# A hybrid decoder layer on one core: a quarter of memory and the spread of ln_g given to GpSimd's queue, other tiles for the first pair, another planning estimate

## The chip, the core and the metric

The kernel runs on one core of one Trainium2 chip, in one launch. The metric is the device time of one execution in microseconds (us). A profiled execution gives the span from the first to the last instruction and a trace of every engine: TensorE (PE, with its weight loads as PEld), VectorE (DVE), ScalarE (ACT), GpSimd (POOL) and SyncE (SP), which only issues transfers.

## The reference, cut to what matters

One pre-norm layer over x (1024 tokens x 2048), all in float32:

- h = RMSNorm(x) * ln_g; P = h @ W_in (2048 x 6672), its columns divided among three groups.
- Group A: chunked causal gMLP gating. Group B: a gated DeltaNet with 8 heads of 128, with a short convolution on q, k, v and a chunked delta rule (64 tokens a chunk), which needs the inverse of a unit lower triangular matrix for each chunk. Group C: cross-attention into 256 memory tokens (4 heads x 128), where m = RMSNorm(mem) * mem_norm_g and the keys and values are m @ w_mem_kv (2048 x 1024).
- Each group's output is multiplied by SiLU of its own gate columns; x + concat(A, B, C) @ W_out; and a final RMSNorm with final_g.

## The kernel before, in words

**Arithmetic.** Every large product is made of three fp32r products of parts: each operand is split into a rounded part and a rest ("hi" by a ScalarE copy, "lo" by a VectorE subtraction, `split_to`, line 440), and `triple` multiplies hi*hi, hi*lo and lo*hi into one PSUM bank. Part of the projections is made from seven products in place of eight of half-size blocks (`seven`, line 1286).

**Order.** All operations are first recorded in a plan (`Plan`, from line 50). `add` finds dependences by tile and region; `price` (from line 180) gives each operation a cost and, for a transfer, a latency `o.lat` behind its last byte; `issue` (line 228) then replays a list schedule with these estimates and emits the instructions of each engine in the order of their estimated start. The chip runs each engine's instructions in that fixed order and waits on semaphores for data. `rank` sets a priority, `behind(op)` lets the planner place an operation only after another one; it is no wait on the chip. As all instructions are emitted from one line, every row of the profile names L295.

**Start.** The memory's 256 rows come in two row tiles (`mem_rows`, kT and qT tiles) of four column quarters of 128x512 each; `load_mem(q)` (line 493) loads quarter q of both. `load_kv(k)` loads row block k of w_mem_kv (512 KB) into one of four buffers: two `wraw`, two `ut`. `spread_mem(q)` (line 539) transposes a quarter on TensorE and splits it into gt (hi) and inv (lo). The loop over k = 0..15 (from line 585) then multiplies block k, scaled by mem_norm_g, into the key banks (acc, 256 columns wide) and the value banks (dn, 512 wide). Between these steps the rows of x come in, are squared and summed, scaled by ln_g (`prep`, line 555, reads the gain tiles `gb`, which lie in the `zg` tiles) and transposed.

The loads at the start are issued in this order on SP's queue: quarter 0 of memory, weight block 0 in two halves, block 1, quarter 1, blocks 2 and 3, quarters 2 and 3. ln_g comes as four rows of 1x512 on ScalarE's queue, and `spread_gain` (line 550) multiplies each with a row of ones on TensorE to spread it over 128 partitions, and copies the bank to `gb` on ScalarE.

**First pair.** After the projections of the first DeltaNet heads, `blocks(0, ...)` starts the seven-product stage. It works in pairs of row blocks: the left operand is loaded into a buffer of `araw` (line 1247) by `loaded`, the right one into `wraw2`, and they are split into `ah4`/`al4` and `whi3`/`wlo3` (line 1249). `raws` lies on tiles of the projections (alo1), `whi`/`wlo` are the tiles that the projections' weights use, `zh`/`zl` lie on the `zg` tiles. The E tiles (two, 128x512) are used before by the DeltaNet's decay matrices.

**Scans.** `inverse` (line 957) makes the triangular inverses of 4 head pairs in 31 steps on VectorE, writes them to DRAM (`tdrearly`, `udrearly`) by GpSimd's queue; `levels` (line 984) reads blocks of them back by GpSimd's queue into `tblk` and `ut` and joins them by small TensorE products (dn<-tblk,gt and dn<-ut,y). Such operations stand between the large products of the seven-product stage.

Of the kernel before, what the change touches and what calls it, by code (L numbers as in the profile page):

```python
# [10 lines left out]
F32R = mybir.dt.float32r  # L11
# [6 lines left out]
P = 128  # L18
# [4 lines left out]
HT = 512  # L23
# [37 lines left out]
class Plan:  # L61
# [27 lines left out]
    @contextmanager  # L89
    def rank(self, cls):  # L90
        old, self.cls = self.cls, cls
        yield
        self.cls = old

    @contextmanager
    def behind(self, op):
        old, self.gate = self.gate, op
        yield
        self.gate = old
# [87 lines left out]
    def price(self, o, name, outs, ins):  # L187

        out = outs[0]
        n = math.prod(out.shape[1:])  # L190
        both = [*outs, *ins]
        psum = any(i.space == PSUM for i in both)
        pointer = any(i.shape[-1] == 1 and math.prod(i.shape[1:]) == 1 for i in ins[1:])
        o.moves = o.lock = 0
        o.lat = 0.0
        if name == "dma_start":
            o.cost = {"sp": 440.0, "act": 430.0, "pool": 550.0}[o.eng]
            src = ins[0]
            run = 4 * min(out.shape[-1], src.shape[-1])
            fixed, byte = self.PACKET  # L200
            o.moves = 4 * math.prod(out.shape) / run * (fixed + byte * run) / self.QUEUES
            if o.eng == "pool":
                o.lat = 1500.0
            elif out.space == DRAM:
                o.lat = 3000.0 if run < 512 else 1500.0
            elif list(src.ap)[0][0] == 0:
                o.lat = 3500.0
        elif o.eng == "pe":
            passes = 1 if ins[0].dtype == F32R else 2 if name == "transpose" else 4
            o.cost = max(13.3 + n / 2.4 * passes, 222.0 if passes == 4 else 110.0) if out.shape[0] == P else 30.0  # L210
            o.lat = 175.0
        elif o.eng == "act":
            o.cost = (165.0 if psum else 200.0) + 0.82 * n + (105.0 if pointer else 0.0)
            o.cost += 190.0 if "accum_out" in o.kw else 0.0
        elif o.eng == "dve":
            n = max([n] + [math.prod(i.shape[1:]) for i in ins])
            o.cost = (n + 151) / 0.96 + (60.0 if pointer and name == "scalar_tensor_tensor" else 0.0)
            o.lock = not psum and (name.startswith("tensor_") or name == "scalar_tensor_tensor")
            o.lock = o.lock and name != "tensor_reduce"
        else:  # L220
            o.lock = 1
            if name in ("memset", "affine_select"):
                o.cost = 100.0 + 0.83 * n * (1 if name == "memset" else 1.4)
                o.lat = 800.0 if name == "affine_select" else 0.0
            else:
                o.cost = 750.0 + 150.0 * (n - 1) if n < 8 else 200.0 + 2.1 * n
# [72 lines left out]
def kernel(  # L299
# [21 lines left out]
    x, mem, w_in, out = x[0], mem[0], w_in[0], out[0]  # L321
# [7 lines left out]
    V, S, G, PE, Q = R.dve, R.act, R.pool, R.pe, R.sp  # L329
    rank, behind = R.rank, R.behind  # L330

    def C(shape, name, dt=F32):
        return sb.tile(list(shape), dt, name=name, tag=name)[:]
# [31 lines left out]
    def heir(old, name, tag, n=4 * HT, dt=F32):  # L365

        t = sb.tile([P, n], dt, name=name, tag=tag)[:]
        R.users[t.tensor.name] = []
        R.heir[t.tensor.name] = old.tensor.name
        return t  # L370
# [23 lines left out]
    kvhi, kvlo = [*whi.bufs], [*wlo.bufs]  # L394
# [4 lines left out]
    ring = {t: Slots(t, 4, [P, HT]) for t in ("kT", "qT", "vs", "kd", "ai")}  # L399
# [3 lines left out]
    zgb = ring["zg"].bufs  # L403
# [23 lines left out]
    ident, ones, utri = (C([P, P], n) for n in ("ident", "ones", "utri"))  # L427
# [55 lines left out]
    def row_tiles(tag):  # L483
        if tag in ("inv", "gt", "ut"):
            return [b[:, i * HT : (i + 1) * HT] for b in (ring[tag](), ring[tag]()) for i in range(2)]
        return [ring[tag]() for _ in range(4)]

    gb = [ring["zg"]() for _ in range(4)]
    kvraw += [ring["ut"]() for _ in range(2)]
    mem_rows = [row_tiles("kT"), row_tiles("qT")]  # L490
    x_rows = {}

    def load_mem(q):
        for mt in range(2):
            Q.dma_start(mem_rows[mt][q], mem[mt * P : (mt + 1) * P, q * HT : (q + 1) * HT])

    def kv_parts(k):
        n = XW if k == 0 else 2 * XW
        return [slice(i, i + n) for i in range(0, 2 * XW, n)]

    def load_kv(k):
        for sl in kv_parts(k):
            Q.dma_start(kvraw[k % 4][:, sl], w_mem_kv[k * P : (k + 1) * P, sl])
# [10 lines left out]
    with rank(2):  # L514
        load_mem(0)
        S.dma_start(mrow, mem_norm_g[0].rearrange("(c p) -> c p", p=P))
        for c in range(4):
            S.dma_start(gb[c][0:1], ln_g[0:1, c * HT : (c + 1) * HT])
        for k in range(4):
            load_kv(k)  # L520
            if k == 1:
                load_mem(1)
    with rank(3):
        load_mem(2)
        load_mem(3)
# [4 lines left out]
    def spare():  # L530
        turn["dn"] = 1 - turn["dn"]
        return flip[turn["dn"]]

    pt = spare()
# [4 lines left out]
    def spread_mem(q):  # L539
# [6 lines left out]
            with rank(2):  # L546
                split_to(h[:, :, sl], l[:, :, sl], tok(tp), V)
        return h, l

    def spread_gain(c, pt):  # L550
        PE.matmul(pt, ones[0:1], gb[c][0:1], start=True, stop=True)
        with rank(3):
            S.copy(gb[c], pt)

    def prep(tt, put, bank):

# [28 lines left out]
    kvmark = []  # L585
    mhl = [spread_mem(0)]
    mhl.append(spread_mem(1))
    for k in range(KT):
        mh, ml = mhl[k // 4]
        if k >= 4:  # L590
            with rank(3):
                load_kv(k)
        hi, lo = kvhi[k % 2], kvlo[k % 2]
        with rank(2):
            for sl in kv_parts(k):
                raw = kvraw[k % 4][:, sl]
                S.activation(hi[:, sl], raw, AF.Copy, scale=gcol[:, k : k + 1])
                V.scalar_tensor_tensor(lo[:, sl], raw, gcol[:, k : k + 1], hi[:, sl], op0=ALU.mult, op1=ALU.subtract)
        kk = k % 4
        for h in range(NX):  # L600
            sl = slice(h * P, (h + 1) * P)
            triple(ka[h][:, :NMEM], (hi[:, sl], lo[:, sl]), (mh[:, kk], ml[:, kk]), k == 0, k == KT - 1)
        for mt in range(2):
            sl = slice(mt * P, (mt + 1) * P)
            triple(va[mt], (mh[:, kk, sl], ml[:, kk, sl]), (hi[:, XW:], lo[:, XW:]), k == 0, k == KT - 1)
        kvmark.append(R.ops[-1])
        if 1 < k < 6:
            spread_gain(k - 2, spare())
        if k in (3, 7):
            mhl.append(spread_mem(k // 4 + 2))  # L610
        if k == 1:
            load_x(0, "vs", kvmark[1:2] * 4)
        if k == 4:
            load_x(1, "kd", kvmark[4:5] * 4)
        if k == 5:
            prep(0, put0(0), spare)
            for mt in range(2):
                rm.append(C([P, 1], f"rm{mt}"))
                V.tensor_copy(rm[mt], row_scale(mem_rows[mt]))
        if k == 7:  # L620

            dg, rmb = (ring["E"]()[:, 0:NMEM] for _ in range(2))
            for mt in range(2):
                V.tensor_scalar(dg[:, mt * P : (mt + 1) * P], ident, rm[mt], None, op0=ALU.mult)
            pt = spare()
            PE.matmul(pt[:, 0:NMEM], ones, dg, start=True, stop=True)
            S.copy(rmb, pt[:, 0:NMEM])
        if k == 9:
            prep(1, put0(1), spare)
            load_x(2, "kT", (kvmark[6], kvmark[7], kvmark[7], kvmark[8]))  # L630
        if k == 13:
            load_x(3, "qT", (kvmark[10], kvmark[11], kvmark[11], kvmark[12]))
            with rank(2):
                prep(2, put0(2), spare)
# [37 lines left out]
    pt = dnr()  # L672
# [44 lines left out]
    def over(bufs):  # L717
        r = Ring("", 0, None)
        r.bufs = bufs
        return r  # L720
# [524 lines left out]
    ob = over(obs)  # L1245
    more = halves(ywide[3])
    araw = over([[t] for t in (*raws, more[0])])
    wraw2 = over([*kvraw[:2], more[1]])
    whi3 = over([*kvhi, heir(zgb[0], "zh", "zg0", 2 * HT, F32R)])
    wlo3 = over([*kvlo, heir(zgb[1], "zl", "zg1", 2 * HT, F32R)])  # L1250
    kept = [[ring[tag](slot=k) for k in range(2)] for tag in ("kT", "qT", "kd", "ai")]
    vs01 = [ring["vs"](slot=k) for k in range(2)]
    for tag in ("kT", "qT", "vs", "kd", "ai"):
# [9 lines left out]
    def load2(ts, src):  # L1263

        for i, x_ in enumerate(src):
            t = ts[i] if len(ts) == 2 else ts[0][:, i * HT : (i + 1) * HT]
            Q.dma_start(t, x_)
        return ts
# [49 lines left out]

    def loaded(src):
        with rank(4):  # L1320
            raw = load2(araw(), src)
        return split2(raw, ah4(), al4())

    def h_left(m, js):
# [456 lines left out]
```

## Time and profile before

| what | value |
|---|---|
| median of 3 runs | 1645.29 us (lowest 1644.62, one run at 8354.71) |
| the profiled execution's own time | 1643.28 us |
| its span | 1641.5 us |
| granted TensorE clock, mean | 0.997 |
| PE busy | 1616.7 us, 98% |
| DVE, ACT, POOL busy | 1258.1, 1031.8, 292.6 us |
| DMA | 427.89 MB, 261 GB/s mean |

Busy time of PE is the time in which at least one matmul is in flight. A matmul's row gives its start and the time until it leaves the array; matmuls overlap, so the distance between two starts, and not the duration, is what one more of them costs. A row of the waits names the engine that waited, what it waited for, the total, how often, and the longest.

### The profile page before, as it was taken

What the parts mean: (1) busy time and instruction counts of PE and PEld (TensorE: products, weight loads), DVE (VectorE), ACT (ScalarE), POOL (GpSimd) and SP (SyncE); (2) the same over time, 40 slices, a digit from 0 to 9 for tenths busy, and PEclk for the clock granted to TensorE, in tenths of its full rate; (3) what the DMA queues carried; (4) which work ended last, traced back from release to release, by engine and by line L of the source; (5) the groups of instructions that cost most, each with busy time, mean ns of one, the idle gap of its engine ahead of it and who ended that gap; (6) DMA issues with size and microseconds to landing.
All of it is one profiled execution on the core that took longest, in us unless ns stands there. A gap on an engine that the chain in (4) does not pass through costs nothing.

```text
span 1641.5 us, 26099 instructions
## 1 busy us (share of the span) xinstructions
PE 1616.7 (98%) x8570; PEld 1354.2 (83%) x8570; DVE 1258.1 (77%) x2081; ACT 1031.8 (63%) x2226; POOL 292.6 (18%) x482
## 2 busy tenths in 40 slices
PE   8999999999999999999999999999999999999997
PEld 6888888887788888888888888888888888888886
DVE  4856777779756668899998887677767788789775
ACT  5957675765465457977775357676656775344345
POOL 0101220351442010313244053301000000000001
PEclk9999999999999999999999999999999999999999
DMA  7887798898986787689888896698788769688646
GB/s 254 255 228 192 224 307 256 240 298 309 352 278 209 258 278 228 209 269 351 287 267 262 291 289 228 195 305 305 251 287 269 241 211 352 221 266 303 219 144 240
DMA packets 278579, 427.89 MB, mean 261 GB/s; under 512 B 30830, under 2 KB 104103, under 8 KB 278443
## 3 DMA queue, kind: packets, MB, share of 16 engines
q1 hardware_dynamic: 255682, 365.76, 68.4%
q0 software_dynamic: 22144, 59.40, 11.6%
q8 instruction: 67, 1.10, 0.3%
q10 hardware_dynamic: 616, 1.07, 0.2%
q14 instruction: 70, 0.57, 0.1%
HBM read 338.52 MB, written 87.06 MB: 259 GB/s over the span
## 4 chain that ended last, share of the span: by engine, by line
PE 81%; DMA 5%; DVE 2%; issue 2%; POOL 1%; ACT 1%; SPq 0%; POOLq 0%; DVEq 0%; ACTq 0%
PE acc L295 62%; PE dn L295 19%; DMA raws<-h0d 1%; DMA el<-vd 1%; DMA pd<-y 1%; DMA tdrearly<-inv 0%; DVE y L295 0%; DMA tblk<-mixd 0%; DMA late<-qT 0%; POOL inv L295 0%; DMA tblk<-tdrearly 0%; DMA ut<-udrearly 0%; DMA y<-in_w_in_dram 0%; DMA vs<-od 0%; DVE inv L295 0%
## 5 line engine op out<-in xcount | busy, mean ns | idle before, releaser
L295 PE MATMUL acc<-ahi,wlo 128*128 128x512 f32 (+1 forms) x1152 | 451.6, 392 | 1.0 <-DVE wlo L295 1.0
L295 PE MATMUL acc<-ahi,whi 128*128 128x512 f32 (+1 forms) x1152 | 449.6, 391 | 1.2 <-ACT whi L295 1.2
L295 PE MATMUL acc<-alo,whi 128*128 128x512 f32 (+1 forms) x1152 | 450.1, 391 | 0.0
L295 PEld LDWEIGHTS acc<-ahi,whi 128*128 128x128 f32 x1152 | 216.6, 188 | 42.4 <-ACT whi L295 1.6
L295 PEld LDWEIGHTS acc<-ahi,wlo 128*128 128x128 f32 x1152 | 216.8, 188 | 41.5 <-DVE wlo L295 1.4
L295 PEld LDWEIGHTS acc<-alo,whi 128*128 128x128 f32 x1152 | 216.7, 188 | 41.1
L295 PE MATMUL acc<-ahi,zh 128*128 128x512 f32 x736 | 232.2, 394 | 0.0
L295 ACT CAST whi<-wraw 128x512 fp32r<-128x512 f32 (+1 forms) x170 | 137.0, 808 | 111.3 <-PE acc L295 85.2
L295 DVE TENSOR_TENSOR wlo<-wraw,whi 128x512 fp32r<-128x512 f32 (+1 forms) x170 | 156.9, 924 | 61.3 <-ACT whi L295 54.9
L295 DVE TENSOR_TENSOR alo<-raws,ahi 128x1024 fp32r<-128x1024 f32 x131 | 159.9, 1221 | 35.9 <-ACT ahi L295 35.5
L295 ACT CAST ahi<-raws 128x1024 fp32r<-128x1024 f32 x131 | 137.3, 1048 | 65.3 <-PE dn L295 28.1
L295 PEld LDWEIGHTS acc<-ahi,zh 128*128 128x128 f32 x736 | 136.7, 188 | 26.9
L295 PE MATMUL acc<-ahi,zl 128*128 128x512 f32 x368 | 144.3, 392 | 0.0
L295 POOL TENSOR_TENSOR small<-small,mhalf 128x1 f32<-128x1 f32 x26 | 17.3, 671 | 591.2 <-DVE small L295 591.1
L295 DVE TENSOR_TENSOR ahi<-y,ahi 128x1024 fp32r<-128x1024 f32 x65 | 79.4, 1221 | 15.3 <-ACT ahi L295 15.2
L295 ACT CAST ahi<-y 128x1024 fp32r<-128x1024 f32 x65 | 68.1, 1048 | 29.9 <-PE dn L295 11.4
L295 PEld LDWEIGHTS acc<-ahi,zl 128*128 128x128 f32 x368 | 69.2, 188 | 13.7
L295 ACT CAST zh<-wraw 128x1024 fp32r<-128x1024 f32 x36 | 37.8, 1050 | 44.2 <-PE acc L295 36.0
L295 DVE TENSOR_TENSOR wlo<-y,whi 128x1024 fp32r<-128x1024 f32 x34 | 41.6, 1223 | 24.8 <-ACT whi L295 23.3
L295 PE MATMUL dn<-wlo,ahi 128*128 128x512 f32 x152 | 59.0, 389 | 0.0
L295 PE MATMUL dn<-whi,alo 128*128 128x512 f32 x152 | 59.0, 389 | 0.0
L295 PE MATMUL dn<-whi,ahi 128*128 128x512 f32 x152 | 58.8, 389 | 0.0
(410 smaller groups left out, 3299.9 us busy)
## 6 DMA issues: line engine op xcount, KB each, us to landing
wraw<-in_w_in_dram SPq DMA_DIRECT2D x268, 256.0 KB, 3.8
raws<-sd SPq DMA_DIRECT2D x148, 256.0 KB, 4.2
y<-in_w_in_dram SPq DMA_DIRECT2D x92, 256.0 KB, 4.7
y<-sd SPq DMA_DIRECT2D x77, 256.0 KB, 4.2
wraw<-in_w_out_dram SPq DMA_DIRECT2D x64, 256.0 KB, 4.2
raws<-h0d SPq DMA_DIRECT2D x54, 256.0 KB, 5.2
y<-in_w_out_dram SPq DMA_DIRECT2D x33, 256.0 KB, 4.6
sd<-zg SPq DMA_DIRECT2D x32, 256.0 KB, 4.7
```

The costliest lines, as they stand in the source:

```text
L295: o.fn(*o.args, **o.kw)
```

## The change

Five edits:

1. Quarter 1 of memory is loaded from GpSimd's queue, as its first instructions, in place of SP's fifth and sixth transfers.
2. The four 1x512 loads of ln_g on ScalarE's queue, the eight TensorE products and the four ScalarE copies that spread them are gone. Four transfers on GpSimd's queue, each reading 512 elements for 128 partitions, fill `gb` instead; the planner may place them only behind step k = 2.
3. The first pair's left operand goes into the two E tiles; later pairs use `araw` as before, so each of its buffers is met one pair later.
4. The hi and lo tiles of the right operands rotate in another order: the `zg` tiles (zh, zl) first, then the second and the first of the projections' tiles.
5. The planner's latency of a transfer on GpSimd's queue is 2500 ns in place of 1500.

The diff, whole:

```
@@ price
             if o.eng == "pool":
-                o.lat = 1500.0
+                o.lat = 2500.0
@@ loads
-    def load_mem(q):
+    def load_mem(q, queue=Q):
         for mt in range(2):
-            Q.dma_start(mem_rows[mt][q], mem[mt * P : (mt + 1) * P, q * HT : (q + 1) * HT])
+            queue.dma_start(mem_rows[mt][q], mem[mt * P : (mt + 1) * P, q * HT : (q + 1) * HT])
@@ start
         load_mem(0)
         S.dma_start(mrow, mem_norm_g[0].rearrange("(c p) -> c p", p=P))
-        for c in range(4):
-            S.dma_start(gb[c][0:1], ln_g[0:1, c * HT : (c + 1) * HT])
+        load_mem(1, G)
         for k in range(4):
             load_kv(k)
-            if k == 1:
-                load_mem(1)
@@ spread_gain
-    def spread_gain(c, pt):
-        PE.matmul(pt, ones[0:1], gb[c][0:1], start=True, stop=True)
-        with rank(3):
-            S.copy(gb[c], pt)
@@ loop over k
         kvmark.append(R.ops[-1])
-        if 1 < k < 6:
-            spread_gain(k - 2, spare())
+        if k == 2:
+            with rank(2), behind(kvmark[-1]):
+                for c in range(4):
+                    G.dma_start(gb[c], ln_g[0, c * HT : (c + 1) * HT].partition_broadcast(P))
@@ first pair
     araw = over([[t] for t in (*raws, more[0])])
+    first_raw = [ring["E"].bufs]
     wraw2 = over([*kvraw[:2], more[1]])
-    whi3 = over([*kvhi, heir(zgb[0], "zh", "zg0", 2 * HT, F32R)])
-    wlo3 = over([*kvlo, heir(zgb[1], "zl", "zg1", 2 * HT, F32R)])
+    whi3 = over([heir(zgb[0], "zh", "zg0", 2 * HT, F32R), *kvhi[::-1]])
+    wlo3 = over([heir(zgb[1], "zl", "zg1", 2 * HT, F32R), *kvlo[::-1]])
@@ loaded
-            raw = load2(araw(), src)
+            raw = load2(first_raw.pop() if first_raw else araw(), src)
```

## The prediction

> **What bounds the kernel now.** I read the page first, then the chain, then PE's waits, then stretches of 41 us, and at last the timeline where PE stands.
>
> ```profile
> span 1641.5 us, 26099 instructions
> PE 1616.7 (98%) x8570; PEld 1354.2 (83%) x8570; DVE 1258.1 (77%) x2081; ACT 1031.8 (63%) x2226; POOL 292.6 (18%) x482
> ```
> ```profile
> PE dn L295 <- DMA y<-in_mem_norm_g_dram: 4.2, 1, 4.2
> PE acc L295 <- ACT whi L295: 1.4, 2, 1.2
> PE dn L295 <- DMA ut<-udrearly: 1.4, 1, 1.4
> PE dn L295 <- DMA kT<-in_mem_dram: 1.4, 2, 1.1
> PE dn L295 <- DVE ai L295: 1.3, 2, 1.0
> PE acc L295 <- DVE wlo L295: 1.2, 2, 1.0
> PE dn L295 <- ACT ut L295: 1.1, 1, 1.1
> PE dn L295 <- DVE ut L295: 1.0, 1, 1.0
> PE acc L295 <- ACT gt L295: 0.9, 1, 0.9
> PE acc L295 <- DVE tn L295: 0.8, 1, 0.8
> PE dn L295 <- DMA el<-vd: 0.6, 1, 0.6
> PE dn L295 <- DMA tblk<-tdrearly: 0.6, 2, 0.3
> ```
> ```profile
> 0.00:41.00 41.00, 34.50 (x182) 28.39 (x182) 18.17 (x25) 23.86 (x42) 1.91 (x10) 0.96 0.76 254
> 41.00:82.00 41.00, 40.59 (x282) 36.42 (x281) 35.35 (x61) 38.87 (x81) 4.99 (x8) 1.00 0.89 255
> 1599.00:1640.00 41.00, 34.06 (x151) 27.88 (x149) 24.26 (x40) 23.75 (x40) 4.81 (x8) 0.95 0.70 252
> ```
>
> PE is busy for 1616.7 of 1641.5 us. All its idle time is 24.8 us: 4.2 before the first transfer lands, 6.9 at the end (41.0 less 34.06, the last row), and some 13 in short waits. So the ceiling is low: what shortens the kernel is matmul work taken away, or one of these waits; everything else must stay hidden. The columns of the stretches are length, busy us of PE, PEld, DVE, ACT and POOL, clock, DMA share and GB/s. After the first stretch PE hardly waits, so a lead won at the start is carried to the end, as long as ACT (38.87 of 41 us in the second stretch) follows.
>
> **The change part by part.**
>
> *Spreading ln_g (edit 2).* It goes from PE and ACT. On ACT the four copies and four issues lie beside PE's work and are counted as nothing; they only give ACT some room.
>
> ```profile
> 15.45 1.98 PE L295 MATMUL dn<-zg,ones 1*128 1x512 f32 x4
> 17.36 0.39 PE L295 MATMUL acc<-gt,whi 128*128 128x256 f32 x1
> L295 PE MATMUL dn<-zg,ones x8: 587/587/692, 15.5 to 32.2; 1*128 1x512 f32 x8
> ```
> ```profile
> 14.64:18.05 3.41, 3.41 (x13) 1.73 (x12) 1.28 (x1) 2.22 (x3) 0.00 (x0) 1.00 0.95 376
> 18.05:21.46 3.41, 3.41 (x18) 3.41 (x17) 0.00 (x0) 0.01 (x1) 0.00 (x0) 0.50 0.67 203
> 21.46:24.87 3.41, 3.41 (x22) 3.02 (x22) 0.69 (x1) 1.15 (x1) 0.00 (x0) 1.00 0.74 262
> ```
>
> The first four hold PE from their start to the next product, 17.36 - 15.45 = 1.91 us; there are eight: **-3.8**. PE's waits name no other operand at this place, so nothing else keeps PE there. Right behind the first four the granted clock falls to 0.50 for 3.41 us, and is 1.00 before and after. At half clock that stretch does 1.7 us less work. The stretch before it holds only 13 matmuls, among them the four that use one row of the array. Whether it is these that lower the clock, the trace doesn't say: the price lies between 0 and -1.7. I take **-1.7**, as the stretch without such products (21.46 to 24.87) has the full clock.
>
> *GpSimd's six transfers (edits 1, 2).* In the built order the two memory loads are GpSimd's first instructions, and the four loads of ln_g follow its memsets with no wait ahead of them: the planner holds them back behind k = 2, the chip does not. So 6 x 256 KB, 1.57 MB, run beside SP's first loads, of which 1.05 MB are new.
>
> ```profile
> L295 POOL DMA_DIRECT2D late<-kT x16: 539/546/607, 139.7 to 845.1; - x16
> 1.19 0.29 POOL L295 TENSOR_SCALAR_AFFINE_SELECT ident<-ident 128x128 f32<-128x128 f32 x1
> E<-gcd POOLq DMA_DIRECT2D x16, 256.0 KB, 7.2
> L295 DVE SCALAR_TENSOR_TENSOR vs<-vs,small,zg x4: 744/748/752, 32.9 to 36.5; 128x512 f32<-128x512 f32 x4
> 10.80 1.09 PE L295 MATMUL dn<-ident,kT 128*128 128x128 f32 x4 [1.12 <-DMA kT<-in_mem_dram]
> ```
> ```profile
> 0.00:4.20 4.20, 0.00 (x0) 0.00 (x0) 0.00 (x0) 0.00 (x0) 1.35 (x9) 1.00 0.42 108
> 4.20:7.61 3.41, 2.23 (x9) 1.71 (x10) 1.29 (x3) 3.02 (x5) 0.00 (x0) 1.00 0.95 309
> 7.61:10.77 3.16, 2.08 (x6) 1.35 (x6) 2.20 (x4) 1.72 (x2) 0.00 (x0) 1.00 0.86 274
> 10.77:15.45 4.68, 4.65 (x20) 4.19 (x20) 1.98 (x3) 1.17 (x2) 0.00 (x0) 1.00 1.04 410
> ```
>
> Two issues of 0.55 us (the first row: the time that one holds GpSimd) delay the identity, ready at 1.48, to 2.6. Its first user waits until 4.2, so this costs nothing; without that cover, 1.1. The gains land some 7 us behind issue (as E<-gcd, the nearest broadcast) at about 13, needed at 32.9: hidden.
>
> Memory and weights are another matter. Length times rate of the rows, added up, gives 0.45 MB moved by 4.2 us, 1.5 by 7.61, 2.4 by 10.77 and 4.3 by 15.45. If both queues take equal turns, the first weight half (the third of SP's 256 KB loads, 0.79 MB with it) lands when 1.57 MB have moved, at about 7.9; its split takes 0.7, and the first product starts near 8.9 in place of 7.61. But the wait of 1.12 us for quarter 1 is gone, and four transposes of it (1.1 us) come ahead of that product. PE's work in the two last rows, 2.08 + 4.65 less these 1.1, ends at 8.9 + 5.6 = 14.5, against 15.45 now. Quarter 2 stands behind 2.6 MB of SP's and all of GpSimd's, 4.2 MB: at 15.2, some 0.7 late for where the built order wants it. I take **0** for the sum of both. Bounds: -1.4 (the two waits for kT vanish, nothing else is late) and +3.4 (the 1.05 new MB at 309 GB/s, all ahead of PE).
>
> [...]
>
> *First pair (edits 3, 4).*
>
> ```profile
> 353.41 0.41 DVE L295 TENSOR_TENSOR ai<-dn,E 128x256 f32<-128x256 f32 x1
> 378.09 1.77 SPq L295 DMA_DIRECT2D raws<-h0d  x4
> 384.61 1.05 ACT L295 CAST ahi<-raws 128x1024 fp32r<-128x1024 f32 x1 [1.56 <-DMA raws<-h0d]
> 386.34 0.39 PE L295 MATMUL acc<-alo,whi 128*128 128x512 f32 x1
> 386.57 0.39 PE L295 MATMUL acc<-ahi,wlo 128*128 128x512 f32 x1
> 388.12 0.50 PE L295 MATMUL acc<-ahi,whi 128*128 128x512 f32 x1 [1.17 <-ACT whi L295]
> 390.81 0.50 PE L295 MATMUL acc<-ahi,wlo 128*128 128x512 f32 x1 [1.02 <-DVE wlo L295]
> ```
>
> Today the first pairs' left operands are loaded at 378.09, when PE has left alo1, land at 384.61, and PE waits 1.17 and 1.02 us for the splits. The E tiles are last read at 353.41 + 0.41, so the new wait of SP's queue for them, with weights behind it, costs nothing at the place where the built order has the two loads (the second near 356); if it came early, every weight behind would be late by as much. One pair is 24 products at 0.23 us (386.57 less 386.34), 5.4 us, enough to cover the second pair's splits, which arrive as now. **-2.2**, bounds -2.2 and 0.
>
> *Estimate (edit 5).* It moves what reads GpSimd's transfers behind other work. In the built order 244 products of 512 columns, in place of 185, stand between the first pair and the first product on tblk: 59 x 0.23 = 13 us more room.
>
> ```profile
> L295 DVE TENSOR_TENSOR alo<-raws,ahi 128x1024 fp32r<-128x1024 f32 x131 | 159.9, 1221 | 35.9 <-ACT ahi L295 35.5
> ```
>
> The inverse on DVE gets three more such splits (1.2 us each) and a few half-size sums between its steps, some 6 us. So 7 us of room meet waits of 1.4 and 0.6 (ut, tblk): **-1.9**, bounds -1.9 and 0. The other waits (ai 1.3, ACT ut 1.1, DVE ut 1.0, tn 0.8, el 0.6: 4.8) are dealt anew; I take no change, bounds -4.8 and +4.8.
>
> **Sum.** -3.8 - 1.7 + 0 - 2.2 - 1.9 = -9.6. The profiled execution's own time is 1643.28 (span 1641.5 and 1.8 around it): 1633.7. The median of the runs lies 2.0 above it, at 1645.29: **1635.7 us**, 0.6% less, which counts as no change: about 2% (33 us) is what a measurement of this kernel can tell.
>
> **Rivals.**
>
> *Transfers in turn.* The new bytes come ahead of the weights, +3.4, and PE, waiting longer in the first 15 us, also gets no better clock (0 for 1.7): -3.8 + 3.4 - 2.2 - 1.9 = -4.5, **1640.8**. For it: DMA share 0.86 to 1.04 in the rows from 4.2 to 15.45. Against: the share covers waiting packets too, and the rate could still rise from 309 to 410.
>
> *Waits only move.* The pair and the levels find another late operand, 0 for 2.2 and 1.9: -5.5, **1639.8**. For: DVE and ACT are dense there, and each new order deals new waits. Against: the room counted above.
>
> *Slower: the first 82 us become bound by transfers.* Both stretches run at 255 GB/s with 0.76 and 0.89 of the DMA engines' time taken. If they hold no more, 1.05 MB cost 4.1 us; the rows of x come late by that, ACT stands in order at their squares with the weights' splits behind, and has 2.1 us of slack in 41. Then the stage ends 4.1 us later, the lead of 5.5 is lost, SP's queue is late at the first pair too (0 for 2.2), and only the levels gain: +4.1 - 1.9 = +2.2, **1647.5**. It decides from the point where the DMA share of 0 to 82 us reaches 1. Against: single rows reach 410 GB/s.
>
> *The change doesn't do what it says:* quarter 1 is no sooner on its way to the products. If it takes as long as the broadcasts (7.2), it lands at 1.9 + 7.2 = 9.1, and since its transposes (1.1) now stand ahead of the first product, that starts at 10.2 in place of 8.9: +1.3, **1637.0**. For it: this is the first use of that queue. Against: nothing else is in flight on it.
>
> **How the numbers follow.** Forecast 0.43, transfers in turn 0.17, waits only move 0.18, slower 0.13, quarter 1 late 0.06, anything else 0.03: the forecast because each of its terms has a row, the others lower as each needs a second thing to go wrong. The low end is the forecast with -1.4 for the start and -4.8 for the other waits: 1629.5; the high end holds the slower case: 1648.0. Faster by over 2% would need more than all idle time and is given 0.01; slower by over 2% needs a new stall of 33 us, for which no row speaks: 0.02; within 2%: 0.97.
>
> **What would show it.** Right: no dn<-zg rows; granted clock 1.00 from about 15 us on; in PE's waits no kT over 1, no whi or wlo at the first pair, no ut or tblk of "early"; PE busy near 1613. Wrong: idle time of PE over 3 us between 5 and 16 us, waits of ACT's jk for in_x in the second stretch, or waits on GpSimd's loads at the levels.

## The result, and the profile after

The changed kernel's median is 1639.07 us (18 runs, 1635.85 to 1644.99), beside 1646.85 us for the kernel before in the same rounds: a ratio of 0.9957, 95% interval [0.9946, 0.9968]. A second set on another chip gave 1639.76 beside 1645.60, 0.9973 [0.9961, 0.9984]. Pooled, the medians are 1639.36 (30 runs) and 1645.87 (46 runs of the kernel before): 6.5 us less. The forecast was 1635.7, 3.4 us below the first median and inside its range; but the range, 1629.5 to 1648.0, also holds the kernel before, and two rivals (1639.8 and 1640.8) lie nearer.

The profiled execution took 1637.3 us. Its page, and PE's longest waits:

```profile
span 1635.5 us, 26085 instructions
PE 1611.9 (99%) x8562; PEld 1353.5 (83%) x8562; DVE 1259.8 (77%) x2082; ACT 1028.6 (63%) x2223; POOL 293.0 (18%) x488
```
```profile
PE dn L295 <- DMA kT<-in_mem_dram: 4.2, 3, 2.2
PE dn L295 <- DMA y<-in_mem_norm_g_dram: 3.7, 1, 3.7
PE dn L295 <- issue: 1.6, 1, 1.6
PE dn L295 <- ACT ut L295: 1.3, 1, 1.3
PE dn L295 <- DVE ai L295: 1.2, 1, 1.2
PE acc L295 <- ACT whi L295: 1.1, 3, 0.5
```

PE is busy for 4.8 us less, and idle for 23.6 us in place of 24.8: most of the 6.0 us of the span is busy time. Of it 3.8 are the products that spread ln_g (four calls in the program, eight instructions in the trace); the rest is mostly the clock at the start (see below). The waits for ut and tblk of "early" and for wlo are gone. In their place stand 4.2 us for kT (1.4 before) and two waits at the levels. The start in the trace (start, duration, engine, operation, and the idle time ahead of it):

```profile
8.37 1.09 PE L295 MATMUL dn<-ident,kT 128*128 128x128 f32 x4 [1.84 <-DMA kT<-in_mem_dram]
10.00 0.58 PE L295 MATMUL acc<-gt,whi 128*128 128x256 f32 x1 [0.54 <-ACT whi L295]
17.80 0.64 PE L295 MATMUL dn<-ident,kT 128*128 128x128 f32 x4 [2.23 <-DMA kT<-in_mem_dram]
1.31 0.72 POOL L295 DMA_DIRECT2D kT<-in_mem_dram  x1 [0.81 <-POOLq L1762]
3.71 2.18 POOL L295 DMA_DIRECT2D zg<-in_ln_g_dram  x4
```
```profile
0.00:41.00 41.00, 32.32 (x199) 28.67 (x200) 21.10 (x29) 24.80 (x43) 6.26 (x17) 1.00 0.88 298
41.00:82.00 41.00, 39.98 (x284) 36.35 (x284) 36.12 (x68) 38.19 (x82) 3.36 (x7) 1.00 0.92 269
7.50:15.00 7.50, 6.09 (x29) 5.45 (x30) 3.61 (x6) 3.57 (x6) 0.00 (x0) 1.00 1.02 382
15.00:22.50 7.50, 5.27 (x39) 4.77 (x39) 2.23 (x4) 2.20 (x2) 0.00 (x0) 1.00 1.02 372
```

GpSimd issues the four ln_g loads at 3.71, held by nothing, as forecast. The 16 DMA engines are then full (share 1.02) from 7.5 to 22.5 us, and PE, which in the kernel before hardly waited behind 11 us, stands for 2.23 us at quarter 2.

Waits alone don't give the price of a stage, as PE may come to them sooner. A better measure is the time at which the same work is done. The order of PE's products differs between the kernels, but at some places the same products have been issued up to there, only in another order. One such place is product 1602 (counted from PE's first, without those that spread ln_g), some 70 us ahead of the first pair. First the kernel before, then the changed one:

```profile
315.92 0.39 PE L295 MATMUL acc<-alo,whi 128*128 128x512 f32 x1
311.76 0.39 PE L295 MATMUL acc<-alo,whi 128*128 128x512 f32 x1
```

The changed kernel is 4.2 us ahead here, of 6.0 us at the end. At product 263, near 55 us, it was 4.6 us ahead.

### The profile page after: what moved, and what is told of

It reads as the page before. It is cut to its first block, busy times and chain, and to the rows that moved or that the text cites. A ratio compares the mean times of both kernels' runs of the same rounds, so it can differ in the third digit from the quotient of the medians.

```text
span 1635.5 us, 26085 instructions
## 1 busy us (share of the span) xinstructions
PE 1611.9 (99%) x8562; PEld 1353.5 (83%) x8562; DVE 1259.8 (77%) x2082; ACT 1028.6 (63%) x2223; POOL 293.0 (18%) x488
## 4 chain that ended last, share of the span: by engine, by line
PE 88%; DMA 7%; DVE 2%; issue 1%; ACT 1%; SPq 0%; POOL 0%; POOLq 0%; DVEq 0%; ACTq 0%
PE acc L295 67%; PE dn L295 21%; DMA y<-in_w_in_dram 2%; DMA kT<-in_mem_dram 1%; DMA wraw<-in_w_in_dram 1%; DMA raws<-h0d 1%; DMA kd<-in_w_in_dram 0%; DMA ut<-in_x_dram 0%; DMA el<-vd 0%; DVE wlo L295 0%; DMA gd<-y 0%; SPq L295 0%; DVE y L295 0%; DMA y<-h0d 0%; ACT whi L295 0%
## 5 line engine op out<-in xcount | busy, mean ns | idle before, releaser
L295 PE MATMUL acc<-ahi,whi 128*128 128x512 f32 (+1 forms) x1512 | 535.1, 392 | 1.3 <-ACT whi L295 0.6
L295 PE MATMUL acc<-alo,whi 128*128 128x512 f32 (+1 forms) x776 | 303.2, 391 | 0.0
L295 PEld LDWEIGHTS acc<-alo,whi 128*128 128x128 f32 x776 | 146.3, 189 | 27.5 <-DVE alo L295 0.2
L295 PE MATMUL acc<-ahi,zh 128*128 128x512 f32 x376 | 148.6, 395 | 0.3 <-ACT vs L295 0.3
L295 PE MATMUL acc<-alo,zh 128*128 128x512 f32 x376 | 148.9, 396 | 0.0
L295 DVE TENSOR_TENSOR ahi<-raws,ahi 128x1024 fp32r<-128x1024 f32 x65 | 79.8, 1228 | 19.0 <-ACT ahi L295 18.8
L295 DVE TENSOR_TENSOR alo<-y,ahi 128x1024 fp32r<-128x1024 f32 x65 | 79.4, 1221 | 18.5 <-ACT ahi L295 18.4
L295 DVE TENSOR_TENSOR alo<-raws,ahi 128x1024 fp32r<-128x1024 f32 x65 | 79.4, 1221 | 15.3 <-ACT ahi L295 15.2
L295 PEld LDWEIGHTS acc<-alo,zh 128*128 128x128 f32 x376 | 70.8, 188 | 13.4
L295 PE MATMUL acc<-whi,ahi 128*128 128x512 f32 x232 | 80.2, 392 | 0.0
```

What stands on the lines that cost most here:

```text
L295: o.fn(*o.args, **o.kw)
```

## The experiments

**Holding ln_g back.** Does the start pay for ln_g's bytes? A copy ahead of the four loads makes GpSimd's queue wait for a weight half; all else keeps its order.

```
         if k == 2:
             with rank(2), behind(kvmark[-1]):
+                G.tensor_copy(gb[0][:, 0:8], lo[:, 0:8])
                 for c in range(4):
                     G.dma_start(gb[c], ln_g[0, ...].partition_broadcast(P))
```

> The changed kernel with one GpSimd copy of 128x8 elements, from the low half of k = 2's weights, put ahead of the four ln_g loads, so that GpSimd's queue really holds them until that half exists (about 15 us). Every other instruction stays in its place. Theory (bytes ahead): after the change the 16 DMA engines are full from 2.5 to 22.5 us (share 0.96 to 1.04), and the 1.05 MB of ln_g stand ahead of the memory quarters and weights; held back, PE's waits for kT fall from 0.18 + 1.84 + 2.23 = 4.2 us to 1.5 or less, the product on k = 0 starts 0.5 to 1.5 earlier, and the time falls by 2 to 3.5 us from 1639.1, to 1636 +- 1. Rival (queue order): quarter 2 is late because SP issues it late, whoever else loads; then the waits for kT stay at 4 +- 0.5 and the time at 1639 +- 1.

Measured: 1638.67 us (12 runs), 0.9968 [0.9955, 0.9981].

```profile
27.15 0.39 PE L295 MATMUL acc<-gt,whi 128*128 128x256 f32 x1 [2.23 <-ACT whi L295]
391.82 0.79 PE L295 MATMUL acc<-ahi,whi 128*128 128x512 f32 x1 [4.47 <-ACT whi L295]
```
```profile
22.33 0.63 ACT L295 ACTIVATE jk<-vs 128x512 bf16<-128x512 f32 x1 [1.84 <-DMA vs<-in_x_dram]
24.37 0.63 ACT L295 ACTIVATE jk<-vs 128x512 bf16<-128x512 f32 x1 [1.31 <-DMA vs<-in_x_dram]
```

The waits for kT fell to 0.75 us and quarter 2 was in time. But ln_g, issued at 15.5, now met the first rows of x: ACT waited for them at its squares, the weights' split stood behind, and PE waited 2.23 us at 27 us. So the hold only moved the cost, and the fall of 2 to 3.5 us did not come. (This profiled execution took 1645.94 us: a 4.47 us stall at the first pair came on top.)

**Quarter 1.** Back on SP's queue, with ln_g early and with ln_g held:

```
-        load_mem(1, G)
         for k in range(4):
             load_kv(k)
+            if k == 1:
+                load_mem(1)
```

> The changed kernel with edit 1 undone: quarter 1 is loaded from SP's queue, behind the weights of k = 1; ln_g still comes early from GpSimd. Theory (bytes ahead): the same bytes move in the same time, only in another order; the first product starts earlier (8.5 to 9.5 in place of 10.0), quarter 1's wait comes later, and k = 3 ends within 1 us of the changed kernel: 1639 +- 1. Rival (edit 1 carries the start): quarter 1 comes behind ln_g as well, its wait grows beyond the 1.1 us it had in the kernel before to 3 or more, and the time rises by 1.5 or more, to 1640.5 or above.

> Both: ln_g held back until k = 2's low half exists, quarter 1 on SP's queue as in the kernel before. Theory (bytes ahead): the start's waits are those of the kernel before (0.2 + 0.9 + 1.1 = 2.3 us), without the eight products that spread ln_g; 1636.5 +- 1. Beside the run with ln_g held alone it prices edit 1 once its competitor is gone: if edit 1 is worth what the prediction's lower bound had (1.4 us), this is 1 to 2 us longer than that run; rival (the queue of a load is indifferent): within 0.5 us of it.

Measured: 1640.60 (9 runs), 0.9979 [0.9965, 0.9994], and 1638.61 (8 runs), 0.9962 [0.9949, 0.9975]. The run with ln_g held as well has 2.44 us of waits up to 45 us, half of them at x's rows again (1.20 at 27.83). In the other, PE waits 2.37 us for quarter 1 at 12.15 in place of 1.84 at 8.37, and its waits of the start, without the first, add up to 3.50 us (changed kernel: 4.98, and 3.15 in the profile below). With ln_g early neither side held: 1640.60 is above the theory's 1640, and the wait of 2.37 below the rival's 3. With ln_g held the start's waits are near the 2.3 us of the theory, but the time is 2 us longer, and within 0.5 us of the run with ln_g held alone, as the rival had it. The intervals overlap with those of the versions that have quarter 1 on GpSimd's queue: edit 1 is worth 0 within about 2 us.

**The changed kernel once more**, to see what in one profile is chance.

> The changed kernel once more, for the share of chance in one profiled execution: same order of instructions, so the same waits of PE to within 0.3 us each. Theory (half clock is dealt by where the clock's window happens to fall): the stretch of 3.4 us at half clock, which the first profile has at 542 to 546 us, stands elsewhere, is missing or comes twice, and the runs' times follow their mean clock, about 1.6 us for each 0.001. Rival (it belongs to the instructions there): it stands at 542 us again. Time 1639 +- 1.

Measured: 1639.76 us (12 runs). The same waits are found to within 0.4 us, but for the first transfer (4.29 in place of 3.70), quarter 1 (0.55 in place of 1.84) and a wait of 0.70 at 444.70. The wait ahead of quarter 2's transposes (1.96) now ends with the split of a weight block (wlo) and not with quarter 2, and so it does in the four profiles below that have this start (1.78 to 2.48): weights and memory are late together (in the first profile the split ended 0.4 us ahead of quarter 2). The half clock, at one place in the first profile, is at two in this one. Each row below is one stretch, the second of each pair at half clock, first of the first profile, then of this one (length, busy us of PE, PEld, DVE, ACT, POOL, clock, DMA share, GB/s):

```profile
538.77:542.19 3.42, 2.10 (x12) 1.33 (x11) 1.76 (x4) 3.33 (x11) 0.00 (x0) 0.98 0.67 207
542.19:545.60 3.41, 3.41 (x13) 3.00 (x13) 0.88 (x2) 1.04 (x3) 0.00 (x0) 0.52 0.77 273
```
```profile
444.62:448.04 3.42, 1.85 (x11) 1.45 (x12) 3.27 (x5) 3.34 (x9) 0.00 (x0) 1.00 1.07 356
448.04:451.45 3.41, 3.41 (x9) 2.66 (x9) 3.13 (x5) 2.50 (x6) 2.78 (x5) 0.50 1.06 382
```
```profile
541.45 1.42 PE L295 MATMUL dn<-tblk,gt 128*128 128x64 f32 x8 [1.29 <-ACT ut L295]
447.58 1.08 PE L295 MATMUL dn<-tblk,gt 128*128 128x64 f32 x8 [1.56 <-issue]
```

Both follow a stretch in which PE worked little (2.10 busy us of 3.42, and 1.85 of 3.42): the two waits at the levels (last two rows, first profile) lie in them. In the first profile the wait at 447 us brought no half clock, in the second it did. The trace's clock records offer a reason: counted from its first record, the changes of the clock in one profile lie whole multiples of 3.413 us behind it, 1, 2 and 475 of them in the kernel before, 155, 156 and 474 in the changed one; the two stretches at half clock of this profile begin 128 and 156 behind its first record (11.11). A window below is one such length. Counted back from 542.02 in the first profile, a border falls at 446.45, inside the wait (446.02 to 447.58); in the second the window from 444.61 to 448.02 holds the whole wait. So theory and rival were each half right: the place belongs to a thinly worked stretch, and whether it struck at 447 us went with where the border of a window fell, which differs between two executions of one order (446.45 in the one; 444.61 and 448.02 in the other); beyond these two profiles that is not shown. The 30 runs of this kernel go with it: at mean clock 0.997 they took 1638.9 us on average (16 runs), at 0.996 1640.3 (5), at 0.995 1643.5 (6); the fitted slope is 2.1 us for each 0.001 (1.6 was expected). What makes a run wait may lower its clock as well, so this is no pure price; but the clock goes along with some 60% of the runs' variance.

**The kernel before once more.**

> The kernel before once more, for the share of chance in one profile: PE's waits as in its first profile to within 0.4 us each. Theory (a window of 3.4 us in which the array does little is followed by one at half clock, if the window falls right): in the kernel before this comes at 18 us behind the four products of one row, and perhaps behind the waits at 434 to 439, 483 and 784 us; it may be missing this time. Rival (chance alone): half clock at places that have neither a wait nor light products just before. Time 1646 +- 1.

Measured: 1644.26 us (12 runs), 0.9996 [0.9982, 1.0009].

```profile
15.34 0.63 PE L295 MATMUL dn<-wlo,gt 128*128 128x512 f32 x1
15.77 0.63 PE L295 MATMUL dn<-whi,inv 128*128 128x512 f32 x1
16.33 2.26 PE L295 MATMUL dn<-zg,ones 1*128 1x512 f32 x4
18.05:21.46 3.41, 3.41 (x25) 2.85 (x24) 0.85 (x1) 0.89 (x2) 0.00 (x0) 1.00 0.51 163
```

The half clock at 18 us is missing although the four one-row products are there. But they stand elsewhere in the windows: two products of 512 columns still start 0.43 us apart at 15.34, which is half speed, and the trace's first clock record, to the full clock, comes at 16.94, in the middle of the four. In the first profile it came at 14.65, ahead of them. A third profile with these products (edits 3 to 5 alone, below) has the full clock from 13.89 and the half clock again, in the window right behind the four:

```profile
13.89:17.30 3.41, 3.41 (x13) 1.71 (x13) 1.31 (x2) 1.79 (x3) 0.00 (x0) 1.00 1.05 411
17.30:20.71 3.41, 3.41 (x18) 3.41 (x18) 0.40 (x1) 0.43 (x1) 0.00 (x0) 0.50 0.75 240
```

So the theory held: both windows at full clock that hold all of the first four were followed by one at half clock. Its claim that waits repeat to 0.4 us did not hold: PE's wait for ai at 728 us, 0.29 in the first profile, is 3.50 here (and the half clock begins in it, at 726.91). DVE makes ai behind work on a weight block, and waits for that block 3.49 us in place of 0.99, in the same order of instructions (first profile, then this one):

```profile
719.40 1.29 DVE L295 TENSOR_TENSOR wraw<-wraw,kT 128x512 f32<-128x512 f32 x2 [0.99 <-DMA wraw<-in_w_in_dram]
720.55 1.29 DVE L295 TENSOR_TENSOR wraw<-wraw,kT 128x512 f32<-128x512 f32 x2 [3.49 <-DMA wraw<-in_w_in_dram]
728.31 0.58 PE L295 MATMUL dn<-inv 128*128 128x256 f32 x1 [3.50 <-DVE ai L295]
```

**ln_g held to k = 3**, so that it passes between x's first rows and its use (k == 3 in the edit of the first hold). Run twice.

> The changed kernel with the GpSimd copy ahead of the four ln_g loads as in the first held run, but reading the low half of k = 3's weights, so that ln_g is issued near 18 us and lands near 25, behind the first rows of x and before its first use at about 31. Theory (bytes ahead, in the right gap): quarter 2 is in time (wait under 0.5, as with the earlier hold) and ACT's squares of x no longer wait for bytes of ln_g (the 2.23 us that PE waited at 27 us falls under 0.7); PE's waits up to 41 us, the first one left out, come to 2.5 or less, against 5.0 (changed kernel) and 5.8 (held to k = 2); time 1636.5 +- 1. Rival (the bytes cost their time wherever they stand before 41 us): the waits stay at 4 to 6, only elsewhere, and the time at 1638.5 to 1640.

> The run with ln_g held to k = 3 once more, as six undisturbed runs were few. Theory: PE's waits up to 41 us, the first left out, at 1.2 to 2 again, and a time 1.5 to 3 below the changed kernel's 1639.1 to 1639.8. Rival: the gain was chance; 1639 or more.

Measured: 1637.36 us (6 runs), 0.9946 [0.9927, 0.9964], and 1636.57 us (5 runs), 0.9937 [0.9926, 0.9949].

```profile
7.50:15.00 7.50, 7.50 (x48) 7.15 (x48) 5.70 (x7) 4.49 (x6) 0.00 (x0) 1.00 1.03 402
15.00:22.50 7.50, 7.50 (x49) 6.71 (x48) 2.67 (x3) 3.03 (x4) 2.29 (x5) 1.00 0.93 288
25.48 0.39 PE L295 MATMUL acc<-gt,whi 128*128 128x256 f32 x1 [0.75 <-ACT whi L295]
```

These are rows of the second run: PE works 7.50 of 7.50 us where the changed kernel's had 6.09 and 5.27, and the wait at 27 us has shrunk to 0.75. The start's waits are 1.44 and 2.06 us in its two profiles. Both medians lie 1.7 to 3.2 us below the changed kernel's; the second interval lies below that of its second set and just overlaps that of its first; the first overlaps both. At product 263 the two profiles are on average 2.2 us ahead of the six that have the changed start. The theory held, though the order of some 70 products between 31 and 46 us changes with the edit too. It is the shortest version measured.

**One part undone.** The estimate back at 1500 ns, and the first pair's tiles as before:

```
-                o.lat = 2500.0
+                o.lat = 1500.0
```
```
-            raw = load2(first_raw.pop() if first_raw else araw(), src)
+            raw = load2(araw(), src)
... (and whi3, wlo3 in their old order)
```

> The changed kernel with edit 5 undone: the planner counts 1.5 us for GpSimd's transfers again. Theory (the estimate only deals the levels' waits anew): PE's waits between 425 and 560 us come to 2 to 4 us as with 2.5 us (2.9 in the changed kernel), and the time is 1639 +- 1.5. Rival (as predicted: the estimate hides the early level's loads, 1.9 us): waits for ut and tblk from the early loads of 1.5 us or more are back on top of the others, and the time is 1641 or more.

> The changed kernel with edits 3 and 4 undone: the first pair's rows of h0 in raws, first weights' halves in whi and wlo. Theory (the tiles' reuse held the first pair): PE's waits between 380 and 395 us are 1.8 to 2.6 (2.19 in the kernel before; 0.7 to 1.2 in the profiles of the changed order that had no late transfer there), and the time rises by about 1.3, to 1640.5 +- 1. Rival (waits only move): another operand is late by as much in either version; waits there within 0.4 of the changed kernel's and the time within 0.7 of it.

Measured: 1642.20 us (12 runs), 0.9968 [0.9957, 0.9980], and 1640.98 us (9 runs), 0.9968 [0.9953, 0.9982]. The ratios lie between the two of the changed kernel, so neither part alone is shown to matter; the medians are 1.2 to 3.1 us longer. With 1500 ns the time is the rival's (1641 or more), the waits are not; with the old tiles both came out as the theory had them, the waits from 380 to 395 us at its lower edge (1.80). The first three rows are of the first kernel, the others of the second:

```profile
434.94 0.62 PE L295 MATMUL dn<-tblk,gt 32*32 32x32 f32 x26 [0.26 <-DMA tblk<-tdrearly]
439.65 0.21 PE L295 MATMUL dn<-ut,y 32*32 32x32 f32 x1 [0.73 <-DMA ut<-udrearly]
367.94 0.66 PE L295 MATMUL acc<-ident,tn 128*128 128x128 f32 x4 [1.81 <-DVE tn L295]
```
```profile
382.06 0.50 PE L295 MATMUL acc<-ahi,whi 128*128 128x512 f32 x1 [0.91 <-ACT whi L295]
391.70 0.66 PE L295 MATMUL acc<-ident,tn 128*128 128x128 f32 x4 [0.89 <-DVE tn L295]
```

With 1500 ns the waits for the early level's loads are back (0.26 and 0.73), yet all waits from 425 to 560 us are 2.0, against 2.9 with 2500: they change operand, and a new wait of 1.81 stands at 368. With the old tiles the pair itself waits 0.91, and the other 0.89 is another operand's.

**Half of the change alone.**

```
edits 1 and 2: load_mem(1, G), ln_g by partition_broadcast; the rest as before
edits 3, 4, 5: first_raw, the order of whi3 and wlo3, o.lat = 2500.0; the rest as before
```

> The kernel before with edits 1 and 2 alone (quarter 1 and ln_g by GpSimd's queue; first pair and estimate as before). Theory (start pays for the bytes): eight products less, -3.8, and the start's waits longer by 2.2 to 2.7, so -1.3, up to -2.9 if what edits 3 to 5 cost when undone alone is taken from the whole; 1643 to 1645 beside 1646.2 of before. Rival (as predicted): -3.8 and a better clock at 18 us, -5.5, nothing lost at the start; 1640.7.

> The kernel before with edits 3, 4 and 5 alone (ln_g spread by TensorE, quarter 1 on SP's queue). Theory (by the runs that undo one part, these are worth 1.5 for the pair and 2.6 for the estimate): -4.1, 1642 +- 1.5. Rival (the new order deals its waits by chance, and the start carries the gain): -1 or less, 1645 or more.

Measured: 1650.31 us (12 runs), 1.0026 [1.0014, 1.0039], and 1644.33 us (12 runs), 0.9987 [0.9976, 0.9998]. Theory and rival both failed on the first: edits 1 and 2 alone make the kernel longer by about 4 us. The second came out between its two. Rows of the first one's trace:

```profile
695.39 0.69 DVE L295 TENSOR_TENSOR wraw<-kT,wraw 128x512 f32<-128x512 f32 x1 [2.97 <-DMA wraw<-in_w_in_dram]
697.21 0.69 DVE L295 TENSOR_TENSOR wraw<-kT,wraw 128x512 f32<-128x512 f32 x1 [1.13 <-DMA wraw<-in_w_in_dram]
708.54 0.42 DVE L295 TENSOR_TENSOR ai<-dn,E 128x256 f32<-128x256 f32 x1
709.01 0.39 PE L295 MATMUL dn<-inv 128*128 128x256 f32 x1 [2.61 <-DVE ai L295]
726.33 1.10 DVE L295 TENSOR_TENSOR y<-y,vs 128x512 f32<-128x512 f32 x1 [2.47 <-DMA vs<-od]
729.39 1.29 DVE L295 TENSOR_TENSOR y<-y,qT 128x512 f32<-128x512 f32 x2 [1.95 <-DMA y<-in_w_in_dram]
731.41 0.60 PE L295 MATMUL dn<-inv,inv 128*128 128x256 f32 x2 [3.80 <-DVE inv L295]
```

Its start is that of the changed kernel: the waits up to 45 us, without the first, are 2.83, and at product 1602 it is 5.2 us ahead of the kernel before. It loses this lead, and more, behind that place. From 600 us on it waits 10.95 us, against 2.03 and 6.14 in the two profiles of before and 1.72 and 1.66 of the changed kernel. The rows say how. DVE waits 4.1 us for a weight block up to 697 us, then works without a gap and reaches `ai` only at 709 us, with PE waiting; later it waits for two more loads, 4.4 us, and PE for its `inv`. Only those two edits differ from the kernel before: what they move at 20 us makes the planner set another order of PE, DVE and ACT 700 us later. Part of such waits is chance in one execution, as the kernel before once more shows (2.03 and 6.14 with one order); that the median of 12 runs rose is not such chance. That such an order is a draw, and not a consequence that could be read from the edits, is what these runs suggest; it is not shown beyond them.

**The estimate further up**, 3500 ns:

> The changed kernel with the estimate for GpSimd's transfers at 3.5 us in place of 2.5. Theory (a new order, waits dealt anew): no further gain; PE's waits between 360 and 560 us come to 2 to 6 us, at other operands than with 2.5; 1638 to 1643. Rival (more room hides more): the waits on loads and copies at the levels, 2.9 us with 2.5, fall under 1 and the time to 1637.5 or less.

Measured: 1639.00 us (6 runs), 0.9953 [0.9941, 0.9965]. At the levels the waits are 1.0 us, nearly as the rival had it, but the time does not fall and stays in the theory's range: 7.8 us of waits stand from 600 us on. The longest:

```profile
852.55 0.51 PE L295 MATMUL dn<-inv,inv 128*128 128x256 f32 x2 [3.01 <-DVE inv L295]
```

## Why the prediction was right, point by point

The direction, the size class and the bound hold: little can be gained as PE is busy 98% of the time, and most of what was gained is busy time of PE at the start. The sum of -9.6 against the 6.0 of the two profiles (6.5 pooled) is too good by some 3. About 1.5 of these were lost in the first 80 us, the rest from the first pair on. The rival "waits only move", with the whole start (-5.5) and nothing at the pair and the levels, gave 1639.8 and describes the runs best.

- *The start as a whole, -3.8 - 1.7 + 0 = -5.5:* nearly right. At product 263, near 55 us, the six profiles with the changed start (the changed kernel twice, edits 1 and 2 alone, the old tiles, 1500 and 3500 ns) are on average 5.3 us ahead of the three with the start of before (4.1 to 6.3). Some 1.2 us go again up to 76 us, where PE waits 1.0 us for xr, whi and small in place of 0.2 (67 to 70 us), which the prediction had not seen; at product 1602 4.0 are left.
- *Spread matmuls, -3.8:* right. The eight rows are gone.
- *Clock, -1.7:* right as a reason at the start, and incomplete. The half clock follows the four products in two of three profiles; of the five without them that were read in stretches up to 41 us (the changed kernel twice, ln_g held to k = 2, and twice to k = 3) one has it, with ln_g held to k = 2: the clock is 0.85 from 22.5 to 30 us, and a wait of PE of 2.23 us lies there. What was missing: with the changed start the full clock also comes sooner, at 12.96 in place of 14.65 and 11.11 in place of 16.94 in the two pairs of profiles, which is 0.8 and 2.9 us of work by an estimate from these times at half speed. Over the whole kernel the stretches at half clock behind these points only move, to the levels and to ai: there is one in each of the first profiles (that at 18 us counted), and there are two in each of the second ones. So this gain of the start was lost again later.
- *GpSimd's six transfers, 0:* mis-sized as a wait. In the first profiles the waits up to 45 us, without the first, went from 2.51 to 4.98. Over three profiles with the start of before (2.51, 3.31, 3.02) and four with the changed one (4.98, 3.15, 3.34, 2.83) the means are 2.9 and 3.6. So +0.6 to +2.5, within the upper bound of 3.4; the sooner clock paid for it. The sum closes for the first profiles at product 263: 3.8 for the products, 2.6 for the clock, less 1.9 for the waits (the shorter first one counted) make 4.5, and 4.6 was measured (in the second pair of profiles 6.3 and 5.6). The first product started at 10.00, not 8.9 (near 8.0 in the second profile); k = 0 ended near 14.7, as forecast (14.5), but near 12.8 in the second profile; quarter 2 was 2.23 late, not 0.7. The rival "transfers in turn" had the mechanism, full DMA engines (share 1.02 from 7.5 to 22.5 us), and not the price: the start it gave, -0.4, is far from the lead measured. That it is ln_g's bytes that are paid is what the run held to k = 3 shows, by some 2 us. Quarter 1's queue made no difference to the time that these runs can tell (1640.60 beside 1639.07 and 1639.76 with ln_g early, 1638.61 beside 1638.67 with ln_g held), the bytes did.
- *First pair, -2.2:* the waits there went from 2.19 to 0.69 (0.40 and 0.29, the latter for vs); in the second profiles from 1.47 to 0.67. So -0.8 to -1.5; the time with the old tiles could not be told from that of the changed kernel.
- *Levels, -1.9:* the early waits vanished as forecast, but the two later levels took their place. From 400 to 600 us the waits went from 3.16 to 2.85, and in the second profiles from 3.87 to 3.48: -0.3. "Waits only move" was right at this place: the step that failed is that more room for the early level would leave the later ones as they were. The wait put down to "issue" is one for ACT's copy:

```profile
446.46 1.02 ACT L295 COPY ut<-dn 32x128 f32<-32x128 f32 x3
```

  It ends at 447.48, and PE starts at 447.58.
- *Other waits, 0 with +-4.8:* the term that decided the rest. From 4.0 us they fell to 2.9 in the first profiles, and from 7.5 to 3.2 in the second ones. With edits 1 and 2 alone they rose so far that the kernel became slower. The bounds were too narrow for that kernel; that the whole change kept its lead was luck as far as these runs tell.
- *The slower rival* had the right stretch and the wrong consequence: the DMA share of 0 to 82 us is 0.88 and 0.92, and ACT's squares did not wait for x in the second stretch.
- *The signs:* of those for right, the missing rows, the busy time (1611.9 against 1613) and the early level's waits came; kT under 1 did not (1.84 and 2.23), nor did a clock of 1.00 throughout. Of those for wrong, PE's idle time between 5 and 16 us was 3.0, at the limit given. One reading was short: the idle time at the end is 8.4 us and not 6.9, as its row stops 1.5 us ahead of the span's end; no term hung on it.

## What to carry to other kernels

A spread by TensorE of a few KB that becomes a broadcast by DMA trades matmuls for bytes (here eight products, 3.8 us, for 1.05 MB): look for the gap in the transfers in which those bytes pass unseen (held to k = 3, the time was 1.7 to 3.2 us less), and hold the queue there by a real dependence, as a planner's order does not (placed behind k = 2, the loads were issued at 3.71 us). Where a planner orders everything, price the edit in its own stage and give the rest a spread read from several orders, not from one profile's waits. Run the same kernel twice before a wait of a microsecond, or a dip of the clock, is made a term of a sum. And measure a stage by when the same work is done, not by its waits: here the waits grew and the stage still became shorter.

## What the runs showed of the hardware that was not expected

The clock row reads 1.00 at the start, yet products run at half speed there. Products of 256 columns in the kernel before, and in the changed one:

```profile
13.40 0.41 PE L295 MATMUL acc<-inv,whi 128*128 128x256 f32 x1
13.61 0.41 PE L295 MATMUL acc<-gt,wlo 128*128 128x256 f32 x1
```
```profile
12.94 0.29 PE L295 MATMUL acc<-gt,whi 128*128 128x256 f32 x1
13.07 0.28 PE L295 MATMUL acc<-inv,whi 128*128 128x256 f32 x1
```

The starts are 0.21 us apart in the one, up to about 14.4 us, and 0.13 in the other, from 12.9 us on. The first clock records of the two traces stand at 14.65 and 12.96; ahead of its first record the view shows 1.00 for want of one. In four profiles with quarter 1 on GpSimd's queue (the changed kernel twice, ln_g held to k = 3 twice) the full speed begins between 10 and 13.0 us, by the first record or by the distance of the products, in four with quarter 1 on SP's queue (the kernel before twice, edits 3 to 5 alone, quarter 1 put back with ln_g early) between 13.9 and 16.9. So edit 1, which puts quarter 1's transposes ahead of the first product, goes with the full clock some 4 us sooner; that it comes from the denser work there, and not from something else in that order, was not tried. In the times of the runs it can't be found, as edit 1 is worth 0 within 2 us.

Once at full clock, PE falls to half while it still works: once in the profile of the kernel before and once in that of the changed one, for 3.41 us each. The window ahead goes with it in part. In these two profiles 942 windows of 3.413 us at full clock, counted from the first record, have another one behind them in which PE works. The three in which PE was busy for 1.4 to 2.13 us (1.92, 1.98 and 2.09) were followed by half clock once, the 939 fuller ones once, behind the first four one-row products. So a wait can cost more than its length: the wait of 1.3 us for ACT's ut at a level was followed by half clock in four of five profiles (the changed kernel twice, ln_g held to k = 3, ln_g held with quarter 1 on SP's queue; not in the second run held to k = 3), by an estimate from the 3.41 us at half speed some 1.7 us of work each.
